# Turning the k scales and the v tiles through VectorE and DRAM instead of TensorE, in a decoder block on one core

## The chip, the cores and the metric

The kernel runs on one core of a Trainium2 chip. The metric is device time in microseconds of one execution, the median of several runs; lower is better. One further execution was recorded by the hardware profiler, and the lines of the profile come from that one.

## The reference

One layer of a hybrid decoder, 512 tokens, model width 2048, all in float32. The input is normalised (RMS) and projected to head groups: A, eight heads of 64 with three causal dilated attention patterns; B, a gated depthwise convolution of 31 taps over 512 channels; C, 16 query heads of 64 on two key/value heads, sliding window of 128, with sinks. In A and C each head's q and k are RMS-normalised. The parts are concatenated, projected and added to the input; a gated feed-forward layer (width 5632) follows.

```python
h = _rms_norm(x, norm1_g[l])
proj = h @ w_in[l]
aq, ak, av, bu, bg, cq, ck, cv = jnp.split(proj, splits, axis=-1)
aq = _rms_norm(aq.reshape(B, S, A_HEADS, HEAD_DIM), a_q_g[l])
ak = _rms_norm(ak.reshape(B, S, A_HEADS, HEAD_DIM), a_k_g[l])
out_a = _dilated_mixture(aq, ak, av).reshape(B, S, A_WIDTH)
...
x = x + mix @ w_out[l]
h2 = _rms_norm(x, norm2_g[l])
x = x + (jax.nn.silu(h2 @ w_gate[l]) * (h2 @ w_up[l])) @ w_down[l]
```

## The kernel before, in words

Activations are kept with the channel on the partition and the 512 tokens along the row. Every float32 product is made of three products of a fast format: operand and weight are each split into a high part (a cast on ScalarE) and a low part (a subtraction on VectorE), and `mm3` (line 314) adds high x high, high x low and low x high.

The work runs in stages. The first four column tiles of the input projection are made together while the input arrives. Then `project` (line 487) makes one tile of 128 columns after another, in the order of `PROJ` (line 46): cv, ck, cq0, bu2, cq3, cq1, and so on to av3, aq3. One tile takes two weight units of 512 KB, eight pairs of 128-row blocks, 48 matmuls of 128x512. The out projection, the gated layer's two input products and its down product follow; the last two are by far the longest part.

Between the matmuls of the projections stands all the attention work. Its place is set by hand: after each pair of blocks `ticks.tick()` is called, and everything that was put down for that tick with `ticks.after(n, ...)` is issued then. A tick is therefore six matmuls and what else of TensorE's work falls into it. Each engine works off its own instructions in the order in which they were issued. All DMAs of this stage are issued from SyncE's queue, in order; an issue that waits (for a buffer to come free, for data) holds those behind it. Weight loads stand in that queue too, up to five units ahead at first and eight later; the casts of a unit are issued two units before its use.

A tile of q or k goes through `head_scales` (line 575): ScalarE copies the projection out of PSUM (line 578) and squares it, VectorE sums the squares by head and turns them in blocks of 32 (line 587), four DMAs write the sums to DRAM (line 595), one reads them back with the tokens on the partitions (line 600), and GpSimd adds and raises to -1/2 (lines 606 to 608). For q that is all: the scale is applied to the scores. For k (`do_k`, line 640) the eight columns of scales are widened by ScalarE to 128x512 (`widen`, line 646), turned by four TensorE transposes into a PSUM bank (`flip`, line 652), multiplied into k by VectorE (`scale`, line 658), split into high and low (lines 663 and 668), and eight DMAs of 128 KB copy the parts of each head to both halves of the partitions (`twin`, line 673). For v (`do_v`, line 680) VectorE multiplies the projection by the tokens' norm factor on its way out of PSUM (line 682), four TensorE transposes bring the tokens onto the partitions (`flip`, line 684), and ScalarE and VectorE split it (`high`, line 690, `low`, line 696).

`attention` (line 716) then puts down a head's scores (line 731), maxima, exponentials, norms, transposes of the weights (lines 769 and 834) and the product with v (`weigh`, line 852). Where a head begins is the latest of several ticks:

```python
t0 = max(ticks.now + ready, head_at[0], box["q at"] - s1, box["k at"], box["v at"] - at_v)
```

`box["k at"]` and `box["v at"]` are fixed numbers of ticks after the tile's projection; they are not measured. cv and ck serve all 16 C heads (first c0, then c3, c1, c5, c2, c7, c4, c6), ak0 to ak3 and av0 to av3 two A heads each.

Of the kernel before, what the change touches and what calls it, by code (L numbers as in the profile page):

```python
# [9 lines left out]
F32 = mybir.dt.float32  # L10
# [4 lines left out]
ALU = mybir.AluOpType  # L15

P = 128
T = 512
NT = T // P
D = 2048  # L20
KT = D // P
HD = 64
HALF = (slice(0, HD), slice(HD, 2 * HD))
# [12 lines left out]
TAP_PAUSE = (197, 211)  # L36


SD, VD, EV = 7, 4, 1


C_TICKS = (1, 6, 2, 2, 2, 3, 5, 1, 4)
# [74 lines left out]
def kernel(ctx: ExitStack, tc: tile.TileContext, xT, wi, wo, wgu, wd, cst_in, outT):  # L117
    nc = tc.nc
    cp = ctx.enter_context(tc.tile_pool(name="consts", bufs=1))
# [16 lines left out]
    ticks = Ticks()  # L136

    def slot(name, dt=F32, cols=T):
        return sp.tile([P, cols], dt, name=name, tag="s")

    def bank(name, cols=T, pool="banks"):
        return psum[pool].tile([P, cols], F32, name=name, tag="b")
# [51 lines left out]
    for p in GU_ORDER:  # L194
        for m in range(2):
# [4 lines left out]
    bufs = {"A": dict(zip(("21", "11", "s", "22"), ("21a", "22a", "sa", "22b"))),  # L200
            "B": dict(zip(("21", "11", "s", "22"), ("21b", "11", "12", "sb")))}
# [6 lines left out]
    for t, (g, r) in enumerate(DOWN):  # L208
# [7 lines left out]
        for k in ("21A", "11A", "21B", "11B", "22A", "22B", "12A", "12B"):  # L216
            c = k[2]
# [20 lines left out]
        bufs = {c: {"21": b["s"], "s": b["21"], "11": b["22"], "22": b["11"]} for c, b in bufs.items()}  # L238

    splits = {}  # L240
    at = {"entry": 0, "split": 0, "use": 0}
# [95 lines left out]
    b = bank("idle")  # L337
    for i in range(WARM):
        nc.tensor.matmul(b, idle, idle[:, None, :].to_broadcast([P, NT, P]), start=True, stop=True)
    b = idle = None  # L340

    nhalf = cp.tile([P, 8], F32, name="nhalf")
# [3 lines left out]
    ident = cp.tile([P, P], F32, name="ident")  # L346
# [28 lines left out]
    gqk = cp.tile([P, 2], F32, name="gqk")  # L375
# [43 lines left out]
    def token_scale(acc, n, name, b=None):  # L419

        v, r = small(name + "v"), small(name + "r")
        if b is None:

            t, b = bank(name), v
            for i in range(NT):
                nc.tensor.transpose(t[:, i * P:(i + 1) * P], acc[:, i * P:(i + 1) * P], ident)
            nc.vector.tensor_reduce(v, t.rearrange("p (a b) -> p a b", b=P), axis=mybir.AxisListType.X, op=ALU.add)
        else:
            stat_rows(b[:, :, None], acc, ones)
        nc.vector.tensor_scalar(v, b, 1.0 / n, EPS, op0=ALU.mult, op1=ALU.add)  # L430
        nc.gpsimd.tensor_tensor(r, v, nhalf[:, :NT], op=ALU.pow)  # L431
        return v, r
# [46 lines left out]
    c64 = cp.tile([P, NT], F32, name="c64")  # L479
    r1b = slot("r1b")  # L480

    v1, r1 = token_scale(ssum, D, "n1")
# [4 lines left out]
    def project(name):  # L487
        b = bank(name, pool="tiles")
        for half in range(2):
            wh, wl = next_unit()  # L490
            for kk in range(8):
                k = 8 * half + kk
                s = slice(kk * P, (kk + 1) * P)
                mm3(b, wh[:, s], wl[:, s], h_hi[k], h_lo[k], k == 0, k == KT - 1)
                if kk == 3:
                    lows_now()
                if kk % 2 == 1:
                    ticks.tick()
        return b
# [72 lines left out]
            mix[f"b{j}"] = yconv[j]  # L572


    def head_scales(b, name, then):

        raw = slot(name + "raw")
        nc.scalar.copy(raw, b)

        def square():  # L580
            sq = slot(name + "sq")
            nc.scalar.activation(sq, raw, AF.Square)
            ticks.after(1, total, sq)

        def total(sq):
            part = cp.tile([P, NT, NT], F32, name=name + "p", tag="hsp", bufs=3)
            nc.vector.tensor_reduce(part.rearrange("p l b -> p b l"),
                                    sq.rearrange("p (b l c) -> p b l c", b=NT, l=NT),
                                    axis=mybir.AxisListType.X, op=ALU.add, apply_transpose=True)
            ticks.after(1, leave, part)  # L590

        def leave(part):
            d = tc.dram_tile([P, 2 * NT * 2], F32, name=name + "d")
            for a in range(4):
                nc.sync.dma_start(d.rearrange("(l i) (a b) -> i l a b", i=32, a=4)[:, :, a], part[32 * a:32 * a + 32])
            ticks.after(2, back, d)

        def back(d):
            t = cp.tile([P, 2, 2, NT], F32, name=name + "t", tag="hst", bufs=3)
            nc.sync.dma_start(t.rearrange("p h a b -> p (h a b)"), d)  # L600
            ticks.after(2, power, t)

        def power(t):
            r = cp.tile([P, NT, 2], F32, name=name + "r", tag="hsr", bufs=4)
            by_head = r.rearrange("p b h -> p h b")
            nc.gpsimd.tensor_add(by_head, t[:, :, 0], t[:, :, 1])
            nc.gpsimd.tensor_add(r, r, c64[:, :, None].to_broadcast([P, NT, 2]))
            nc.gpsimd.tensor_tensor(r, r, nhalf.rearrange("p (a b) -> p a b", b=2), op=ALU.pow)
            then(r)

        ticks.after(1, square)
        return raw
# [25 lines left out]
        ticks.after(1, high)  # L638

    def do_k(box, b, name, gi):  # L640
        def then(r):
            ticks.after(2, widen, r)

        raw = head_scales(b, name, then)
        box["k at"] = ticks.now + SD + 11
        def widen(r):
            wide = slot(name + "wide")
            nc.scalar.copy(wide.rearrange("p (a b c) -> p a b c", a=NT, b=2),
                           r[:, :, :, None].to_broadcast([P, NT, 2, HD]))
            ticks.after(1, flip, wide)  # L650

        def flip(wide):
            b2 = bank(name + "t")
            for i in range(NT):
                nc.tensor.transpose(b2[:, i * P:(i + 1) * P], wide[:, i * P:(i + 1) * P], ident)
            ticks.after(1, scale, b2)

        def scale(b2):
            k = slot(f"{name}k")
            nc.vector.scalar_tensor_tensor(k, raw, gqk[:, gi:gi + 1], b2, op0=ALU.mult, op1=ALU.mult)  # L660
            ticks.after(1, high, k)

        def high(k):
            hi = slot(f"{name}hi", F32R)
            nc.scalar.copy(hi, k)
            ticks.after(1, low, k, hi)

        def low(k, hi):
            lo = slot(f"{name}lo", F32R)
            nc.vector.tensor_sub(lo, k, hi.bitcast(F32))  # L670
            ticks.after(1, twin, hi, lo)

        def twin(*parts):
            box["k"] = [[slot(f"{name}{'hl'[i]}{h}", F32R) for i in range(2)] for h in range(2)]
            for h in range(2):
                for to, part in zip(box["k"][h], parts):
                    for at in HALF:
                        nc.sync.dma_start(to[at].bitcast(F32), part[HALF[h]].bitcast(F32))

    def do_v(box, b, name):  # L680
        vs = slot(name + "s")
        nc.vector.tensor_mul(vs, b, r1b)

        def flip():
            b2 = bank(name + "t")
            for i in range(NT):
                nc.tensor.transpose(b2[:, i * P:(i + 1) * P], vs[:, i * P:(i + 1) * P], ident)
            ticks.after(1, high, b2.rearrange("p (a b c) -> p a b c", a=NT, b=2))

        def high(src):  # L690
            box["v"] = [slot(f"{name}{h}", F32R).rearrange("p (a b c) -> p a b c", a=NT, b=2) for h in range(2)]
            for h in range(2):
                nc.scalar.copy(box["v"][h][:, :, h], src[:, :, h])
            ticks.after(1, low, src)

        def low(src):
            for h, v in enumerate(box["v"]):
                nc.vector.tensor_sub(v[:, :, 1 - h], src[:, :, h], v[:, :, h].bitcast(F32))

        box["v at"] = ticks.now + VD + 3  # L700
        ticks.after(VD, flip)


    UNITS = {
# [240 lines left out]
    for name in PROJ[HEAD4:]:  # L945
# [4 lines left out]
        b = project(name)  # L950
# [3 lines left out]
        if kind == "c":  # L954
            box = Heads(shared) if j else shared
        else:
            box = boxes.setdefault(j, {})
# [10 lines left out]
    b = box = boxes = shared = None  # L968
# [81 lines left out]
    for half in range(2):  # L1050
        for i, n in enumerate(OUT_ORDER[half]):
            if half == 1 and i == 2:
                open_banks(banks=2, high=2)
            b = bank(f"o{half}_{n}", pool="tiles")
            wh, wl = next_unit()
            for kk in range(8):
                k = 8 * half + kk
# [3 lines left out]
                s = slice(kk * P, (kk + 1) * P)  # L1061
# [18 lines left out]
    b = m_hi = m_lo = r1b = mult_a = bias_a = bias_c = over = upper = None  # L1080
# [33 lines left out]
    flip = [1]  # L1114
# [177 lines left out]
    for g in range(2 * NP):  # L1292
        p, m = GU_ORDER[g // 2], g % 2
# [257 lines left out]
```

## Time and profile before

| | |
|---|---|
| Time, median of 3 runs | 1867.45 us (1867.01 to 1867.95) |
| Profiled execution | 1867.59 us |
| Its span, first to last instruction | 1865.9 us |
| TensorE busy | 1858.8 us |
| VectorE, ScalarE, GpSimd busy | 1446.7, 1330.5, 1141.7 us |
| DMA traffic | 307.38 MB, mean 165 GB/s |
| Stage of the projections with attention | about 50 to 480 us of the span |

The times of the rows below count from the start of the span. A row of a timeline has start, duration, engine, line, operation and tile; in brackets stands how long the engine was idle before it and what ended that. In the list of DMAs the last number is the median time from issue to landing in us. In the chain of the work that ended last, a row is a start, a duration and the engine, tile and line that held the chain.

### The profile page before, as it was taken

The numbers are of one execution on the slowest core, as the hardware profiler recorded it, in microseconds if no ns is written. First come the engines' busy times: TensorE is split into PE (matmuls) and PEld (weight loads), VectorE is DVE, ScalarE is ACT, GpSimd is POOL, SyncE is SP. The second block draws the span as 40 slices with busy tenths as digits, with TensorE's granted clock in tenths as the row PEclk, the third lists the DMA queues.
The fourth block names the chain that finished last, engine by engine and source line by source line (L and its number), as shares of the span: only waits on it lengthen the run. The fifth ranks groups of instructions, "written<-read, shape, count | busy, mean of one in ns | idle before, by whom it ended". The sixth has DMA issues, their size and how long they took to land.

```text
span 1865.9 us, 28280 instructions
## 1 busy us (share of the span) xinstructions
PE 1858.8 (100%) x9606; PEld 1591.2 (85%) x9606; DVE 1446.7 (78%) x2290; ACT 1330.5 (71%) x1840; POOL 1141.7 (61%) x828
## 2 busy tenths in 40 slices
PE   9999999999999999999999999999999999999998
PEld 7888888888888888888888888888888888888887
DVE  6778878998689777777777777777777777777777
ACT  6355644553457878888888888888888877778775
POOL 0125533100013877888878878788787878779775
PEclk9999999999999999999999999999999999999999
DMA  7243253343333455555555655555457867677645
GB/s 273 77 145 90 77 147 96 94 130 120 131 123 113 146 160 158 174 183 158 174 158 171 186 155 178 159 171 185 143 168 249 315 226 237 210 228 234 203 131 113
DMA packets 213328, 307.38 MB, mean 165 GB/s; under 512 B 75200, under 2 KB 124992, under 8 KB 213184
## 3 DMA queue, kind: packets, MB, share of 16 engines
q1 hardware_dynamic: 213040, 305.57, 52.3%
q8 instruction: 76, 1.25, 0.3%
q14 instruction: 68, 0.56, 0.1%
q10 hardware_dynamic: 144, 0.01, 0.0%
HBM read 244.03 MB, written 53.09 MB: 159 GB/s over the span
## 4 chain that ended last, share of the span: by engine, by line
PE 99%; DMA 0%; SPq 0%; DVE 0%; issue 0%; ACT 0%; DVEq 0%
PE out L1146 46%; PE out L1405 7%; PE out L1404 7%; PE out L1406 7%; PE o L317 3%; PE o L315 3%; PE o L316 3%; PE cq L315 2%; PE cq L317 2%; PE cq L316 2%; PE ak L315 1%; PE aq L315 1%; PE av L315 1%; PE aq L317 1%; PE aq L316 1%; PE av L316 1%
## 5 line engine op out<-in xcount | busy, mean ns | idle before, releaser
L1146 PE MATMUL out<-h,wh 128*128 128x512 f32 x2464 | 588.5, 391 | 0.0
L1146 PEld LDWEIGHTS out<-h,wh 128*128 128x128 f32 x2464 | 452.7, 188 | 87.5
L1146 PEld LDWEIGHTS out<-h,wl 128*128 128x128 f32 x2464 | 315.9, 191 | 12.0
L1146 PE MATMUL out<-h,wl 128*128 128x256 f32 x2464 | 319.6, 283 | 0.0
L1404 PE MATMUL out<-wh,a 128*128 128x512 f32 x620 | 240.4, 388 | 0.0
L1405 PE MATMUL out<-wl,a 128*128 128x512 f32 x620 | 240.3, 388 | 0.0
L1406 PE MATMUL out<-wh,a 128*128 128x512 f32 x620 | 240.3, 388 | 0.0
L286 ACT CAST wh<-w 128x1024 fp32r<-128x1024 f32 (+2 forms) x94 | 96.8, 1031 | 151.0 <-PE o L316 62.8
L264 DVE TENSOR_TENSOR wl<-w,wh 128x1024 fp32r<-128x1024 f32 (+2 forms) x95 | 113.2, 1191 | 41.1 <-ACT wh L286 39.5
L1404 PEld LDWEIGHTS out<-wh,a 128*128 128x128 f32 x620 | 116.4, 188 | 24.0
L1406 PEld LDWEIGHTS out<-wh,a 128*128 128x128 f32 x620 | 116.4, 188 | 23.8
L1405 PEld LDWEIGHTS out<-wl,a 128*128 128x128 f32 x620 | 116.4, 188 | 23.8
L1414 DVE TENSOR_TENSOR y<-y,out 128x512 f32<-128x512 f32 x164 | 106.2, 683 | 25.7 <-PE out L1406 23.8
L526 DVE SCALAR_TENSOR_TENSOR y<-bu,cst,y 128x511 f32<-128x511 f32 (+14 forms) x120 | 90.0, 750 | 0.7
L315 PE MATMUL o<-mh_c,wh 128*128 128x512 f32 x128 | 51.1, 399 | 0.0
L315 PE MATMUL cq<-hh,wh 128*128 128x512 f32 x128 | 50.5, 395 | 0.0
L317 PE MATMUL o<-mh_c,wl 128*128 128x512 f32 x128 | 50.0, 391 | 0.0
L316 PE MATMUL cq<-hl,wh 128*128 128x512 f32 x128 | 49.9, 390 | 0.0
L316 PE MATMUL o<-ml_c,wh 128*128 128x512 f32 x128 | 49.9, 390 | 0.0
L317 PE MATMUL cq<-hh,wl 128*128 128x512 f32 x128 | 49.9, 390 | 0.0
L431 POOL TENSOR_TENSOR lvr<-lvv,nhalf 128x4 f32<-128x4 f32 x1 | 1.9, 1923 | 70.7 <-DVE lvv L430 70.7
L182 POOL TENSOR_TENSOR w('s', 'g0')_5667<-w('21', 'g0')_5513,w('22', 'g0')_5511 128x1024 f32<-128x1024 f32 x1 | 2.5, 2454 | 69.0 <-DVE wl L264 69.0
(3062 smaller groups left out, 4941.6 us busy)
## 6 DMA issues: line engine op xcount, KB each, us to landing
od<-a SPq DMA_DIRECT2D x154, 256.0 KB, 4.7
a<-od SPq DMA_DIRECT2D x154, 256.0 KB, 5.5
w<-in_wi SPq DMA_DIRECT2D x58, 512.0 KB, 3.5
w<-in_wo SPq DMA_DIRECT2D x32, 512.0 KB, 3.5
x<-in_xT SPq DMA_DIRECT2D x16, 256.0 KB, 7.1
xr<-in_xT SPq DMA_DIRECT2D x16, 256.0 KB, 3.8
x2d<-xr SPq DMA_DIRECT2D x16, 256.0 KB, 2.0
z<-x2d SPq DMA_DIRECT2D x64, 64.0 KB, 3.8
```

The source lines that it names most:

```text
L182: nc.gpsimd.tensor_add(out[:, :n], raws[key[a]][0][:, :n], raws[key[b]][0][:, :n])
L264: fn(*args)
L286: (nc.vector.tensor_copy if u == 0 else nc.scalar.copy)(hi[:, :n], t[:, :n])
L315: nc.tensor.matmul(out, wh, xh, start=start, stop=False)
L316: nc.tensor.matmul(out, wh, xl, start=False, stop=False)
L317: nc.tensor.matmul(out, wl, xh, start=False, stop=stop)
L526: nc.vector.scalar_tensor_tensor(yconv[j][:, i:], hconv[j][:, :T - i], c, yconv[j][:, i:], op0=ALU.mult, op1=ALU.add)
L1146: nc.tensor.matmul(out, lhs[:, s], rhs, start=begin, stop=x is xs[-1] and low == flip[0], skip_group_check=True)
L1404: nc.tensor.matmul(b[:, lo:hi], x[:, high], wh[:, s], start=start, stop=False, skip_group_check=True)
L1405: nc.tensor.matmul(b[:, lo:hi], x[:, high], wl[:, s], start=False, stop=False, skip_group_check=True)
L1406: nc.tensor.matmul(b[:, lo:hi], x[:, low], wh[:, s], start=False, stop=last, skip_group_check=True)
L1414: getattr(eng, op)(t, t, src)
```

## The change

For k, GpSimd writes the eight scales of a token (heads first) into the head of a zeroed 32-column block; VectorE turns that block in pieces of 32x32; four DMAs write the pieces' eight useful rows to DRAM, in rows of 128 bytes, as an array of eight rows of 128 tokens; two DMAs read it back, each one row of 512 tokens of one head spread over 64 partitions. The multiply into k reads that instead of a PSUM bank. From the power to the last copies of k it takes 11 ticks instead of 7, and `box["k at"]` is 21 ticks after the projection instead of 18.

For v, VectorE turns the projection itself in pieces of 32x32 out of PSUM; four DMAs write it to DRAM with tokens as rows, in pieces of 128 bytes; one reads 128x512 back in rows of 512 bytes, and GpSimd multiplies by the norm factor, which now is one number per partition and block. `high` comes seven ticks after the projection instead of five, and `box["v at"]` is ten instead of seven.

All else of the kernel is the same text; lines behind line 575 move by up to 26.

```diff
-SD, VD, EV = 7, 4, 1
+SD, KD, VD, EV = 7, 9, 10, 1
...
         def power(t):
-            r = cp.tile([P, NT, 2], F32, name=name + "r", tag="hsr", bufs=4)
-            by_head = r.rearrange("p b h -> p h b")
-            nc.gpsimd.tensor_add(by_head, t[:, :, 0], t[:, :, 1])
-            nc.gpsimd.tensor_add(r, r, c64[:, :, None].to_broadcast([P, NT, 2]))
-            nc.gpsimd.tensor_tensor(r, r, nhalf.rearrange("p (a b) -> p a b", b=2), op=ALU.pow)
-            then(r)
+            if home is None:
+                r = cp.tile([P, 2, NT], F32, name=name + "r", tag="hsr", bufs=4)
+            else:
+                r = home().rearrange("p (h b) -> p h b", h=2)
+            nc.gpsimd.tensor_add(r, t[:, :, 0], t[:, :, 1])
+            nc.gpsimd.tensor_add(r, r, c64[:, None, :].to_broadcast([P, 2, NT]))
+            nc.gpsimd.tensor_tensor(r, r, nhalf.rearrange("p (h b) -> p h b", h=2), op=ALU.pow)
+            then(r.rearrange("p h b -> p b h"))
...
     def do_k(box, b, name, gi):
+        wide = []
+
+        def home():
+            wide.append(slot(name + "wide"))
+            nc.gpsimd.memset(wide[0][:, 2 * NT:32], 0.0)
+            return wide[0][:, :2 * NT]
+
         def then(r):
-            ticks.after(2, widen, r)
+            ticks.after(2, turn)
-        raw = head_scales(b, name, then)
-        box["k at"] = ticks.now + SD + 11
-        def widen(r):
-            wide = slot(name + "wide")
-            nc.scalar.copy(wide.rearrange("p (a b c) -> p a b c", a=NT, b=2),
-                           r[:, :, :, None].to_broadcast([P, NT, 2, HD]))
-            ticks.after(1, flip, wide)
-
-        def flip(wide):
-            b2 = bank(name + "t")
-            for i in range(NT):
-                nc.tensor.transpose(b2[:, i * P:(i + 1) * P], wide[:, i * P:(i + 1) * P], ident)
-            ticks.after(1, scale, b2)
-
-        def scale(b2):
+        raw = head_scales(b, name, then, home)
+        box["k at"] = ticks.now + SD + KD + 5
+
+        def turn():
+            nc.vector.transpose(wide[0][:, 32:64], wide[0][:, :32])
+            ticks.after(1, leave)
+
+        def leave():
+            d = tc.dram_tile([2 * NT, P], F32, name=name + "e")
+            for a in range(4):
+                nc.sync.dma_start(d[:, 32 * a:32 * a + 32], wide[0][32 * a:32 * a + 2 * NT, 32:64])
+            ticks.after(2, back, d)
+
+        def back(d):
+            rows = d.rearrange("(h b) p -> h (b p)", h=2)
+            for h in range(2):
+                nc.sync.dma_start(wide[0][HALF[h]], rows[h:h + 1].to_broadcast([HD, T]))
+            ticks.after(3, scale)
+
+        def scale():
             k = slot(f"{name}k")
-            nc.vector.scalar_tensor_tensor(k, raw, gqk[:, gi:gi + 1], b2, op0=ALU.mult, op1=ALU.mult)
+            nc.vector.scalar_tensor_tensor(k, raw, gqk[:, gi:gi + 1], wide.pop(), op0=ALU.mult, op1=ALU.mult)
             ticks.after(1, high, k)
...
     def do_v(box, b, name):
-        vs = slot(name + "s")
-        nc.vector.tensor_mul(vs, b, r1b)
-
-        def flip():
-            b2 = bank(name + "t")
-            for i in range(NT):
-                nc.tensor.transpose(b2[:, i * P:(i + 1) * P], vs[:, i * P:(i + 1) * P], ident)
-            ticks.after(1, high, b2.rearrange("p (a b c) -> p a b c", a=NT, b=2))
+        turned = slot(name + "t")
+        nc.vector.transpose(turned, b)
+
+        def leave():
+            d = tc.dram_tile([T, P], F32, name=name + "d")
+            for a in range(4):
+                at = slice(32 * a, 32 * a + 32)
+                nc.sync.dma_start(d.rearrange("(n i) c -> i n c", i=32)[:, :, at],
+                                  turned[at].rearrange("p (n c) -> p n c", c=32))
+            ticks.after(2, back, d)
+
+        def back(d):
+            vs = slot(name + "s")
+            nc.sync.dma_start(vs.rearrange("p (b c) -> p b c", b=NT), d.rearrange("(b p) c -> p b c", p=P))
+            ticks.after(2, scale, vs)
+
+        def scale(vs):
+            by = vs.rearrange("p (a c) -> p a c", a=NT)
+            nc.gpsimd.tensor_mul(by, by, r1[:, :, None].to_broadcast([P, NT, P]))
+            ticks.after(2, high, vs.rearrange("p (a b c) -> p a b c", a=NT, b=2))
...
-        box["v at"] = ticks.now + VD + 3
-        ticks.after(VD, flip)
+        box["v at"] = ticks.now + VD
+        ticks.after(1, leave)
```

2 lines of the change are left out of this document (1 added, 1 removed).

## The prediction

> **What bounds the kernel now.** I read the page first (busy shares, chain that ended last), then what TensorE waited for, then the chain in order of time, and last the timelines of each engine between 55 and 110 us, where the first k and v tiles are made.
>
> ```profile
> PE 1858.8 (100%) x9606; PEld 1591.2 (85%) x9606; DVE 1446.7 (78%) x2290; ACT 1330.5 (71%) x1840; POOL 1141.7 (61%) x828
> ```
> ```profile
> PE 99%; DMA 0%; SPq 0%; DVE 0%; issue 0%; ACT 0%; DVEq 0%
> ```
> ```profile
> PE idle L339 <- DVE ones L349: 1.1, 1, 1.1
> PE sides L1369 <- DVE y L1383: 0.7, 1, 0.7
> PE in L315 <- ACT wh L286: 0.4, 1, 0.4
> ```
>
> TensorE is busy for the whole span and the chain is TensorE for 99% of it. Its only waits are at the two ends; between 60 and 480 us it waits for nothing. So each microsecond of TensorE work that goes is worth a microsecond, and each microsecond for which TensorE is made to wait costs one. All else is cover.
>
> **What is removed.** Ten groups of four transposes (line 655 for five k tiles, line 687 for five v tiles). The chain in order of time prices each; these are the first, the fourth and fifth, and the last of ten:
>
> ```profile
> 68.41 0.44 PE cvt L687 x4
> ```
> ```profile
> 260.78 0.44 PE ak0t L655 x4
> 263.97 0.44 PE av0t L687 x4
> ```
> ```profile
> 389.12 0.44 PE av3t L687 x4
> ```
>
> 10 x 0.44 = **4.4 us less on the path**. The instruction order of the changed kernel has exactly these ten groups fewer and no matmul more. ScalarE also loses a copy per k tile and each v its multiply on VectorE (0.69 us), which a turn of 0.70 us (row below) replaces: both off the path, no gain. The tick times in the order show what moves: the scores of c0 come three ticks later, those of the other early c heads one, from c4 on nothing, and the out projection finds its rows at the same ticks as before.
>
> **What is added.** Per v tile four writes of 64 KB, one read of 256 KB and a GpSimd multiply; per k tile four tiny writes and two reads of 128 KB: 55 issues. They cost SyncE some 25 us at the 0.44 us of a row below. Its queue has cover in general:
>
> ```profile
> SPq L254 <- DVE wl L264: 827.8, 194, 11.0
> ```
>
> What counts is whether a chain of DMAs ends later than TensorE needs it. TensorE needs a k tile first at c0, after cv and ck, where a tick is shortest (no attention work between the matmuls):
>
> ```profile
> 98.43 0.39 PE L315 MATMUL cq<-hh,wh 128*128 128x512 f32 x1
> 98.66 0.39 PE L316 MATMUL cq<-hl,wh 128*128 128x512 f32 x1
> ```
> ```profile
> 99.11 0.22 PE L737 MATMUL c0s<-ckh,cq 128*128 128x128 f32 x1
> 99.17 0.28 PE L738 MATMUL c0s<-ckl,cq 128*128 128x128 f32 x1
> ```
>
> Matmuls start 0.227 us apart, six make a tick: 1.36 us. Three ticks later and two groups of transposes (cv, ck) earlier, c0's scores come up at 99.1 + 4.1 - 0.9 = **102.3 us**. I follow the two chains to that moment.
>
> *The v tile of cv.* In the new order on ScalarE its two casts stand ahead of the copy of ck's projection, and wait for GpSimd's multiply, that for the read, that for the writes.
>
> ```profile
> L1267 DVE STREAM_TRANSPOSE zt<-z x16: 703/704/705, 714.0 to 1298.5; 128x512 f32<-128x512 f32 x16
> ```
> ```profile
> 65.12 0.69 DVE L682 TENSOR_TENSOR cvs<-cv,r1b 128x512 f32<-128x512 f32 x1
> ```
> ```profile
> 89.32 0.74 DVE L660 SCALAR_TENSOR_TENSOR ckk<-ckraw,gqk,ckt 128x512 f32<-128x512 f32 x1
> ```
> ```profile
> 92.44 0.69 DVE L670 TENSOR_TENSOR cklo<-ckk,ckhi 128x512 fp32r<-128x512 f32 x1
> ```
> ```profile
> 68.89 0.65 ACT L693 CAST cv<-cvt 128x256 fp32r<-128x256 f32 x2 [0.93 <-PE cvt L687]
> 73.00 0.59 ACT L578 COPY ckraw<-ck 128x512 f32<-128x512 f32 x1 [3.46 <-PE ck L317]
> ```
> ```profile
> 59.79 2.55 POOL L517 TENSOR_TENSOR bu<-bu,bg 128x512 f32<-128x512 f32 x2 [7.54 <-ACT bg L516]
> ```
> ```profile
> 84.61 1.64 POOL L608 TENSOR_TENSOR ckr<-ckr,nhalf 128x8 f32<-128x8 f32 x1
> ```
> ```profile
> 88.21 1.75 SPq L595 DMA_DIRECT2D cq0d<-cq0p  x4
> 90.01 0.53 SPq L636 DMA_DIRECT2D cq<-cq0l  x1
> 90.58 0.59 SPq L637 DMA_DIRECT2D cq<-cq0l  x1
> ```
> ```profile
> 93.94 1.48 SPq L678 DMA_DIRECT2D ckl<-cklo  x2
> ```
> ```profile
> w<-in_wi SPq DMA_DIRECT2D x58, 512.0 KB, 3.5
> ```
> ```profile
> x2d<-xr SPq DMA_DIRECT2D x16, 256.0 KB, 2.0
> z<-x2d SPq DMA_DIRECT2D x64, 64.0 KB, 3.8
> ```
> ```profile
> y<-x2t SPq DMA_DIRECT2D x16, 256.0 KB, 6.9
> ```
> ```profile
> ckh<-ckhi SPq DMA_DIRECT2D x4, 128.0 KB, 2.8
> ckl<-cklo SPq DMA_DIRECT2D x4, 128.0 KB, 2.7
> ```
>
> The turn stands where the multiply stood: 65.1 to 65.8. Four issues at 0.44 us, the last begun at 67.2. The trace has no such write; the nearest row is z, the same 64 KB in pieces of 128 bytes, four issues in a row, the other way: 3.8 us, so landed at 71.0. The 256 KB read is not in the trace either; between x2d's 2.0 and y's 6.9 the nearest is a weight tile, a DRAM read in this very stage: 3.5 us, landed at 74.5. The multiply takes half of 2.55: 75.8. The casts take 0.65: 76.5. ScalarE could have taken ck's copy at 73.0, so **ck starts 3.5 us late**. Two weight loads are held back behind them on SyncE, by some 5 us; the row above shows such waits of up to 11.0 us that TensorE never felt, so that costs nothing.
>
> *The k tile of ck.* Its square, sum, first trip through DRAM and power stay as they are, so the power ends at 86.25 + 3.5 = 89.8. The turn of 32 columns (between nothing and 0.7; I take 0.2) ends at 90.0. On SyncE follow four writes (1.75), the four of cq0 queued behind them (1.75), the two of line 636/637 (1.15, by their starts and the last's length) and two reads, the second begun at 95.2. 128 KB with 2 KB rows is ckh's row, 2.8 us: **98.0**. VectorE wanted it at tick 31: the old line 655 stood at tick 26, 87.8, so 87.8 - 0.4 + 5 x 1.36 = 94.2. VectorE waits, and behind it stand a gated input, a weight's low half and a tap; unit 21's low half is wanted at tick 40 only. From ckk to the end of cklo the trace has 3.8 us with the same sort of work between (89.32 to 93.13): 101.8. Then two issues of 0.6, the second at 102.5, and 2.7 to land: **105.2**. TensorE stands at c0 since 102.3 and waits **2.9 us**. That is the cost; it isn't made good later, as nothing else bounds the kernel.
>
> *The other eight tiles* I cost at nothing. Ticks last 1.6 us and more there (ak0t at tick 130 and av0t at tick 132 stand 3.2 us apart above), so 6 and 7 ticks give the same chains 10 us; the k tiles wait 7 to 71 ticks for their scores after their last copies, against 3 at ck. The tightest place I found is a0's product with av0, where ak1's low half and av1's two now fall among the VectorE work ahead of it:
>
> ```profile
> 333.79 0.42 DVE L850 TENSOR_TENSOR a0pl<-a0t,a0ph 128x256 fp32r<-128x256 f32 x1
> ```
> ```profile
> 334.92 0.28 PE L864 MATMUL a0o<-a0pl,av 128*128 128x256 f32 x1
> ```
>
> 0.7 us of slack, against some 0.6 us of work moved in (net of what moves out before an idle stretch): 0 to 0.5 us, I take 0.
>
> **Sum.** -4.4 + 2.9 = -1.5. The profiled execution took 1867.59 (span 1865.9 and 1.7 around it), 0.14 above the median of 1867.45; from the median: **1866.0 us**, 0.08% less. About 0.2% (3.7 us) is what a measurement of this kernel can tell from no change.
>
> **Rivals.**
>
> *No wait at c0: 1863.0.* If the v tile's write and read both take x2d's 2.0 us, 3.3 us of the 3.5 go, and with them all 2.9 of the wait; the full 4.4 remain: 1867.45 - 4.4. For it: by the DMA line of the page the second slice (47 to 93 us) is at 0.2, while z and y ran after 700 us, at 0.4 to 0.8. Against it: 512 pieces per write.
>
> ```profile
> DMA  7243253343333455555555655555457867677645
> ```
> Every wait under 0.7 us gives a time that counts as faster.
>
> *The v tile comes much later: 1870.8 to 1872.8, slower.* One place, the queue of ScalarE behind cv's casts. The price is what the two transfers take beyond my values: z's slowest took 5.2 (row below), y's median is 6.9, so 1.4 + 3.4 = 4.8 more: the wait is 7.7, the sum +3.3, 1870.8. It decides from a wait of 8.1 us, that is, from c0's low half landing at 110.4. A dropped clock (next) would add 2.0.
>
> ```profile
> DMA to landing us min/median/max: 3.3/3.8/5.2
> ```
>
> *The wait also drops TensorE's clock: 1868.0.* The trace has TensorE coming out of idleness at its start:
>
> ```profile
> 1.12 3.56 PE L339 MATMUL idle<-idle 128*128 128x512 bf16 x8 [1.12 <-DVE ones L349]
> 4.55 1.47 PE L472 MATMUL in<-hh,wh 128*128 128x512 f32 x4
> ```
>
> Eight matmuls at 0.43 us apart and four at 0.33, against 0.227: 8 x 0.2 + 4 x 0.1 = 2.0 us lost. The same after a wait at c0 gives 1866.0 + 2.0. [...]
>
> *That the change does not do what it says* I leave no chance: the transposes are gone from the order.
>
> **How the numbers follow.** Forecast (wait of 0.7 to 7 us, clock kept) 0.54; no wait 0.26; late v 0.12; dropped clock 0.08. Faster by over 0.2%: 0.26. Slower: 0.12. Within: 0.54 + 0.08 = 0.62. The range goes from no wait, 1863.0, to the late v at full clock, 1871.0; beyond lie parts of the late v (0.1) and extra gain or loss that I can't name.
>
> **What would show it.** TensorE's waits should have one new row, c0's scores (line 763) for a DMA of ckl or ckh, about 2.9 us, and its first score near 105. ck's copy on ScalarE (line 578) should start near 76.5 behind a wait of the casts for GpSimd. The landing of cvd and cvs tests 3.8 and 3.5, that of ckwide 2.8. ckk (line 674) should start near 98.0. TensorE's groups should be ten fewer, the granted clock 1.0 and matmuls after c0 0.227 apart. I am wrong if TensorE waits elsewhere (a0's product, line 890, first), or if ScalarE takes ck's copy at 73 all the same.

## The result, and the profile after

The changed kernel takes **1874.75 us** (median of 7 runs, 1870.12 to 1877.69), the kernel before 1867.45 on the same chip: a ratio of 1.0038, with a 95% interval of 1.0027 to 1.005. The forecast was 1866.0 with a range up to 1871.0; the time lies above it, 7.3 us slower. The profiled execution took 1874.93 with a span of 1873.2, which is 7.3 more than the span of before, so it can stand for the median.

Two lines of its page answer to those of before: busy time of the engines, and the chain that ended last.

```profile
PE 1857.4 (99%) x9566; PEld 1588.8 (85%) x9566; DVE 1449.9 (77%) x2295; ACT 1327.3 (71%) x1835; POOL 1155.5 (62%) x838
...
PE 89%; DVE 5%; DMA 2%; SPq 2%; POOL 1%; issue 1%; ACT 0%; POOLq 0%; DVEq 0%
```

Forty matmul records fewer, as said. But the chain is no longer TensorE alone: a tenth of the span now passes through the other engines, DMAs and SyncE's queue. What TensorE waited for (us in total, times, longest):

```profile
PE o L315 <- DVE xr L1019: 2.5, 2, 1.6
PE c7o L890 <- POOL c7pl L822: 2.1, 2, 1.8
PE c4o L890 <- POOL c4pl L822: 1.8, 2, 1.3
PE c6s L763 <- DMA cq<-cq6l: 1.2, 1, 1.2
PE idle L339 <- DVE ones L349: 1.1, 1, 1.1
PE a1o L890 <- DVE a1pl L876: 1.0, 1, 1.0
PE sides L1395 <- DVE y L1409: 0.7, 1, 0.7
PE c0s L764 <- DMA ckl<-cklo: 0.6, 1, 0.6
```

Rows for `idle` and `sides` are the old ones at the ends. The other six are new: nine waits, 9.2 us. The one that I had forecast, c0's, is the smallest. The large ones stand at products of the c heads (c7o, c4o), at c6's scores and at the out projection, between 250 and 430 us, and none of them waits for a tile that the change makes. So something behind the changed tiles was late. VectorE's waits show the first candidate, a wait for a tile's own trip through DRAM, which the kernel before doesn't make:

```profile
DVE ckk L674 <- DMA ckwide<-cke: 3.9, 1, 3.9
...
DVE ak0k L674 <- DMA ak0wide<-ak0e: 3.5, 1, 3.5
...
DVE ak2k L674 <- DMA ak2wide<-ak2e: 2.8, 1, 2.8
```

In these rows VectorE takes its instructions in order. The multiply into k stands in its queue, and while it waits for the DRAM read, all behind it waits too, other heads' work above all: c7lp below starts at 242.48, though its input c7hp was done on ScalarE at 239.00 and VectorE stood idle for 2.75 us in between. Around ak2 (start, length, idle time before in brackets):

```profile
232.74 0.21 DVE L657 STREAM_TRANSPOSE ak2wide<-ak2wide 128x32 f32<-128x32 f32 x1 [0.90 <-POOL ak2wide L610]
...
237.47 1.48 DVE L526 SCALAR_TENSOR_TENSOR y<-bu,cst,y 128x483 f32<-128x483 f32 x2
241.69 0.75 DVE L674 SCALAR_TENSOR_TENSOR ak2k<-ak2raw,gqk,ak2wide 128x512 f32<-128x512 f32 x1 [2.75 <-DMA ak2wide<-ak2e]
242.48 0.69 DVE L810 TENSOR_TENSOR c7lp<-c7t,c7hp 128x512 fp32r<-128x512 f32 x1
```

From the turn to the landed read it is 9.0 us; VectorE had 6.2 us of other work between the two and then stood 2.75. Right behind stands the low half of c7's weights, c7lp. GpSimd makes c7ph and c7pl of c7's halves, and c7o is the next thing TensorE waits for after c0, at 251.79. (The step between the two is looked at below.)

At ak0 the delay goes on to SyncE. The multiply started at 271.53 after 3.45 of idleness. Behind it on VectorE stand the low half of a weight (274.54), for which a weight load on SyncE waits 6.4 us, and ak0's own low half (276.33). So the eight twin transfers of ak0 (line 692) are issued only from 276.23 on, in one run, and cq6's transfers stand behind them, though their sums were ready at 277.63. c6's scores wait for these:

```profile
268.77 7.36 SPq L254 DMA_DIRECT2D w<-in_wi  x2
276.23 1.12 SPq L692 DMA_DIRECT2D ak0h<-ak0hi  x2
...
280.52 1.10 SPq L692 DMA_DIRECT2D ak0l<-ak0lo  x2
281.72 2.28 SPq L595 DMA_DIRECT2D cq6d<-cq6p  x4
284.11 0.47 SPq L638 DMA_DIRECT2D cq<-cq6l  x1
```

### The profile page after: what moved, and what is told of

It is laid out like the page before. It is cut to its first block, busy times and chain, and to the rows that moved or that the text cites. A ratio compares the mean times of both kernels' runs of the same rounds, so it can differ in the third digit from the quotient of the medians.

```text
span 1873.2 us, 28281 instructions
## 1 busy us (share of the span) xinstructions
PE 1857.4 (99%) x9566; PEld 1588.8 (85%) x9566; DVE 1449.9 (77%) x2295; ACT 1327.3 (71%) x1835; POOL 1155.5 (62%) x838
## 4 chain that ended last, share of the span: by engine, by line
PE 89%; DVE 5%; DMA 2%; SPq 2%; POOL 1%; issue 1%; ACT 0%; POOLq 0%; DVEq 0%
PE out L1172 46%; PE out L1431 7%; PE out L1430 7%; PE out L1432 7%; PE o L315 3%; PE o L317 3%; PE o L316 3%; PE cq L315 1%; PE cq L317 1%; PE cq L316 1%; DVE wl L264 1%; PE in L315 1%; PE in L317 1%; PE in L316 1%; DVE y L526 1%
```

## The experiments

My theory after this, **W**: engines that take their work in order stand waiting for the new DRAM reads, and what is queued behind them, other heads' steps, comes too late for TensorE. The rival **Q**: the 55 issues and their traffic delay other transfers wherever they stand, waits or not. Later came **S** (slots) and **T** (the c heads' shifted ticks). Every kernel ran beside the kernel before on the same chip, whose median there was 1867.4 to 1867.6; the ratio is to that, with its 95% interval.

| run | what it is | us | ratio to before |
|---|---|---|---|
| (changed) | | 1874.75 | 1.0038 (1.0027 to 1.0050) |
| no_turn | before, transposes left out | 1862.29 | 0.9973 (0.9962 to 0.9984) |
| later | changed, A tiles read later | 1865.81 | 0.9993 (0.9984 to 1.0002) |
| k_late | changed, A's k tiles read later | 1866.75 | 0.9999 (0.9991 to 1.0008) |
| v_late | changed, A's v tiles read later | 1873.05 | 1.0029 (1.0020 to 1.0038) |
| k_only | k half of the change | 1870.63 | 1.0018 (1.0009 to 1.0027) |
| v_only | v half of the change | 1866.54 | 0.9994 (0.9986 to 1.0003) |
| extra | before + 55 idle transfers, two slots held | 1876.22 | 1.0045 (1.0031 to 1.0058) |
| extra_t | the same, no slot held | 1869.00 | 1.0007 (0.9998 to 1.0016) |
| slots71 | before with 71 slots | 1869.39 | 1.0010 (1.0001 to 1.0018) |
| ck_te | changed, ck on TensorE | 1873.64 | 1.0033 (1.0022 to 1.0045) |
| a02_te | changed, ak0 and ak2 on TensorE | 1868.47 | 1.0007 (0.9998 to 1.0016) |
| a13_te | changed, ak1 and ak3 on TensorE | 1872.34 | 1.0028 (1.0018 to 1.0038) |
| twin_late | changed, ak1's and ak3's twins later | 1878.53 | 1.0061 (1.0048 to 1.0073) |
| mix | 28 of 40 transposes gone | 1863.88 | 0.9981 (0.9972 to 0.9990) |
| mix_all | 36 of 40 gone | 1869.14 | 1.0010 (1.0001 to 1.0019) |

### later, k_late, v_late: more ticks before the read's user

```diff
 # do_k, A tiles only
-            ticks.after(3, scale)
+            ticks.after(7, scale)
 # do_v, A tiles only
-            ticks.after(2, scale, vs)
+            ticks.after(6, scale, vs)
...
-            ticks.after(2, high, vs...)
+            ticks.after(4, high, vs...)
```

`later` has both edits, `k_late` the first, `v_late` the second; `box["k at"]` and `box["v at"]` move along, and so do the casts and twins behind the multiply.

> The changed kernel with more ticks between a transfer's issue and the instruction that reads it, for the eight tiles of the A heads alone (k: three ticks become seven; v: two become six, and two become four ahead of the casts). Same instructions, same 55 issues. Theory W (engines that take their work in order stand waiting for the DRAM reads: VectorE 2.8 us for ak2wide and 3.5 us for ak0wide, ScalarE 4.3 us behind av0s, and the other heads' steps queued behind them come late): these waits go, and with them TensorE's at c7o, c4o, a1o and the output projection (7.4 us of its 9.2): 1863 to 1867 us. Theory Q (the issues themselves, on SyncE's queue and as DMA traffic, delay other heads' transfers wherever they stand): as the changed kernel, 1870 to 1877.

> The changed kernel with the later multiply (three ticks become seven) for the four k tiles of the A heads alone; v as changed. Tells which of the two kinds of wait made the 8.9 us that the run with both later won. If it is VectorE's wait for ak0wide and ak2wide (6.2 us of idle, with the P halves of c7 and c4 queued behind): most of it, 1866 to 1868 us. If it is ScalarE's and GpSimd's wait at the v tiles: 1872 to 1875. If the two add up to one (each shifts the other's transfers on SyncE): in between, 1868 to 1872.

> The counterpart: later multiply and casts for the four v tiles of the A heads alone; k as changed. If VectorE's wait at k is the cause: VectorE still stands 2 to 4 us at ak2wide and ak0wide, 1871 to 1874 us. If v's is: 1866 to 1868. If shared: 1868 to 1872.

Measured: 1865.81, 1866.75, 1873.05. As W has it: 8.9 us come back with the same 55 issues in place, 8.0 of them by the k tiles' multiply alone. (The times of `later` and `k_late` themselves cannot be told from before's: both intervals include 1.) `later`'s waits of TensorE:

```profile
PE c0s L766 <- DMA ckl<-cklo: 1.6, 1, 1.6
PE idle L339 <- DVE ones L349: 1.1, 1, 1.1
PE a1s L766 <- DMA ak1l<-ak1lo: 1.0, 1, 1.0
PE sides L1397 <- DVE y L1411: 0.7, 1, 0.7
PE a3s L765 <- DMA ak3h<-ak3hi: 0.6, 1, 0.6
```

c7o, c4o, c6s, a1o and o are gone from it. In their place a1 and a3 wait for their own k tiles, which four more ticks bring too late: these heads have no slack. Since the casts and the twins of A's k tiles move too, the time alone doesn't part VectorE's wait from a better place of the twins on SyncE; the rows have to do that.

The step from VectorE's 2.8 us to c7o's 1.8 goes by a detour on GpSimd. cq4's row landed within 0.4 us of the same moment in both kernels; then in the changed one

```profile
243.39 0.29 POOL L608 TENSOR_TENSOR cq4r<-cq4t 128x8 f32<-128x8 f32 x1 [7.59 <-DMA cq4t<-cq4d]
243.76 2.91 POOL L609 TENSOR_TENSOR cq4r<-cq4r,c 128x8 f32<-128x8 f32 x1
...
252.50 0.29 POOL L822 TENSOR_SCALAR_AFFINE_SELECT c7pl<-c7lp 128x128 fp32r<-128x128 f32 x1
```

and in `later`

```profile
243.74 0.20 POOL L608 TENSOR_TENSOR cq4r<-cq4t 128x8 f32<-128x8 f32 x1 [7.68 <-DMA cq4t<-cq4d]
244.02 0.20 POOL L609 TENSOR_TENSOR cq4r<-cq4r,c 128x8 f32<-128x8 f32 x1
...
249.38 0.73 POOL L824 TENSOR_SCALAR_AFFINE_SELECT c7pl<-c7lp 128x128 fp32r<-128x128 f32 x1
```

an addition of eight numbers per partition takes 2.91 us instead of 0.20, and c7pl ends 2.7 us later (252.8 against 250.1). In the changed kernel VectorE was just then working off what had piled up, without a gap from 241.69 on; in `later` it was idle for 1.7 us before 244.94. In the kernel before and in `k_late` VectorE was idle during this addition as well, and it takes 0.20 there too. Why it takes 2.91 beside a busy VectorE, no run shows. Over the kept traces, c7o waits in three kernels alone, the changed one, `v_late` and `k_only`, and in these GpSimd's three instructions for cq4's row take 4.8, 4.5 and 3.8 us, in all others 2.0 to 3.1. In `a13_te` and `twin_late` VectorE stands 2.2 and 2.3 us at ak2 too, but the row takes 2.1 and 2.2 and c7o does not wait. So c7o waits by way of GpSimd; that VectorE's backlog is what held GpSimd up is argued, as no run took the two apart.

c4o's wait has a part of another kind. Ahead of its first piece of c4pl GpSimd stood 2.66 us:

```profile
277.19 0.41 POOL L819 TENSOR_SCALAR_AFFINE_SELECT c4pl<-c4lp 128x256 fp32r<-128x256 f32 x1 [2.66 <-PE c4t L799]
```

It reads c4lp, which was ready at 274.62, and nothing of c4t, so what it stood for is the slot that c4t's input held. In `slots71`, where nothing differs but two missing slots, the same line (for another piece) stands 2.36 us for the same transposes. So the slots that the change's tiles hold have a share in c4o's 1.8 us; `later`, `k_late` and `a02_te` have neither this wait nor c4o's.

### k_only, v_only: each half alone

The other half's functions and ticks are those of the kernel before.

```diff
 # k_only: do_v of before (its flip after 4 ticks); v_only: do_k of before
```

> The k half of the change alone: 30 of the 55 issues, half of the transposes gone (2.2 us). Theory W: VectorE's three long waits (2.8, 3.5 and 3.9 us) are all for k's reads, so most of the loss comes back: 1869 to 1873 us. Theory Q: 30/55 of the 11.9 us that the changed kernel lost beside what it saved, less 2.2: 1867.45 + 6.5 - 2.2 = 1871.7.

> The v half alone: 25 of the 55 issues, the other half of the transposes gone (2.2 us). Theory W: no VectorE wait for a read is left, only ScalarE's and GpSimd's (4.3 us at av0): 1865 to 1868 us. Theory Q: 25/55 of 11.9 us less 2.2: 1867.45 + 5.4 - 2.2 = 1870.7.

Measured 1870.63 and 1866.54. `v_only` fits W alone; `k_only` fits W and Q (1871.7) alike. The k half is the loss, the v half at best a small gain (1.0 of the 2.6 us that its transposes are worth, and its interval includes no change). But 3.1 and -1.0 make 2.1, not 7.3: the halves make each other worse. `k_only`'s waits of VectorE point at one place:

```profile
DVE ak2k L674 <- DMA ak2wide<-ak2e: 2.1, 1, 2.1
...
DVE ak0k L674 <- DMA ak0wide<-ak0e: 1.1, 1, 1.1
```

ak0's wait is 1.1 us without v tiles, 3.5 with: in the changed kernel av0's four writes stand ahead of ak0's four on SyncE (issued from 262.01 and 264.38). This is a likely reason and not a shown one: with the same v tiles ak0's wait was only 1.7 to 2.1 in `ck_te`, `a13_te` and `twin_late`.

### no_turn: what the transposes are worth

```diff
-            b2 = bank(name + "t")
-            for i in range(NT):
-                nc.tensor.transpose(b2[...], wide[...], ident)
-            ticks.after(1, scale, b2)
+            ticks.after(1, scale, wide)
 # and the same in do_v
```

> The kernel before without the 40 transposes and with nothing in their place: VectorE and ScalarE read the unturned tiles from where they lie, at the same ticks. It leaves out the turning itself, and its output is not the reference's. It prices the removal alone: 40 x 0.11 us = 4.4 us of TensorE, so 1863.0 us if TensorE is the bound where they stand; 1867.4 if their time is given back in a wait.

Measured 1862.29, 5.3 us below before (1867.57 there) and 0.7 below what was expected: some 0.13 us per transpose, and nothing is given back in a wait. (In its trace the matmuls of the projections gain 0.47 us on the kernel before at each of the ten groups, 4.7 in all.) So the changed kernel lost 1874.75 - 1862.29 = 12.5 us to its own chains.

### extra, extra_t, slots71: the transfers by themselves

```diff
 # extra: in do_k and do_v of before, at the ticks of the change
+            nc.sync.dma_start(d[...], src[...])          # four writes
+            nc.sync.dma_start(dst[...], ...)             # one read, two for k
 # extra_t: src is the constant bias_a, and
+            dst = slot(name + "x")                       # for each read
 # slots71
-N_SLOTS = 73
+N_SLOTS = 71
```

> The kernel before, transposes and all, plus the change's 55 transfers of the same shapes at the same ticks on SyncE, between a scratch slot and DRAM: nobody reads what they bring. Theory W (only instructions that wait for a transfer cost): TensorE's path is untouched, 1867 to 1869 us. Theory Q (the issues and the traffic cost by themselves): the 11.9 us that the changed kernel lost beside its saving, or the larger part of it: 1873 to 1879 us.

> The kernel before plus the change's 55 transfers for nobody, as in the earlier run of that kind, but without the two scratch slots that run held all along: the writes leave from a constant tile, and each read lands in a slot taken for it alone and free when it has landed. In the earlier run GpSimd stood 8.3 us for a slot that ak0lo's twin transfers (issued 5 us later than in the kernel before) had not freed. Theory S (the two slots made that wait, the issues are free): 1867 to 1869 us. Theory Q (the issues delay the twins, and whoever comes next in a slot waits for them): 1872 to 1877.

> The control: the kernel before with 71 slots for 73, no transfer added. Theory S: most of the 8.7 us of the earlier run with 55 idle transfers, 1872 to 1876. Theory Q: 1867 to 1868.

`extra` at 1876.22 seemed to prove Q. It didn't. GpSimd stood for a slot that ak0's twins held, and TensorE behind it:

```profile
280.50 0.45 POOL L822 TENSOR_SCALAR_AFFINE_SELECT c4pl<-c4lp 128x256 fp32r<-128x256 f32 x1 [8.30 <-DMA ak0l<-ak0lo]
```

Without the two held slots the same 55 transfers cost 1.6 us (interval -0.4 to 3.0), and two slots fewer without any transfer cost 2.0. Neither alone is 8.7; together they are. The row above suggests why: a transfer that is late is harmless until the next user of its slot is near (here GpSimd, which stood 8.30 us for it). For `slots71` both forecasts missed (S too high, Q too low), for `extra_t` S's upper end held. So the issues are nearly free, as forecast, as long as nobody waits for them, and Q doesn't make the loss of the changed kernel. S as such doesn't either, as two slots cost 2.0 us; but what the changed kernel's own extra slots (one more per v tile while it turns) add to it was not tried, and c4o's row above suggests that they add something.

### ck_te, a02_te, a13_te: single tiles back on TensorE

```diff
-            do_k(box, b, name, 1 if kind == "c" else 0)
+            (do_k if name in NAMES else do_k_dram)(box, b, name, 1 if kind == "c" else 0)
 # do_k is that of before, do_k_dram the changed one; NAMES: ck | ak0 ak2 | ak1 ak3
```

> The changed kernel with ck alone back on TensorE, so that the c heads stand at the ticks of the kernel before; 36 transposes gone. Theory W (VectorE's waits for ak2wide and ak0wide): these stay, 1870 to 1874 us. Rival T (the c heads' shift by one to three ticks put c7's P halves behind cq4's row on GpSimd and so made the loss): c7o, c4o and c6s no longer wait, 1865 to 1868.

> The changed kernel with ak0 and ak2 back on TensorE (32 transposes gone); ck, ak1, ak3 and all v tiles as changed. The changed kernel's TensorE waits at c7o, c4o and c6s (5.1 of 9.2 us) stand right behind VectorE's waits for ak2wide and ak0wide. If these two waits are their cause: 5.1 x 11.9/9.2 = 6.6 us come back, 0.9 us of transposes return, 1869 us (1868 to 1870), and o and a1o still wait. If the c waits have another cause (the v tiles, the c heads' ticks): 1873 to 1876.

> The counterpart: ak1 and ak3 back on TensorE, ck, ak0, ak2 and the v tiles as changed. If the waits of o and a1o (3.5 us of 9.2) come from ak1's and ak3's later steps (their twins' issues, 6 us of SyncE, now stand ahead of the read of aq3's row, and VectorE stands 3.5 us for that row): 4.5 us come back, 0.9 return, 1871 us (1870 to 1872), and c7o, c4o, c6s still wait. If o and a1o wait because VectorE is behind since ak2 and ak0: 1874 to 1876.

Measured 1873.64, 1868.47, 1872.34: the first two land in their forecasts, the last one just beside it, and T falls as the cause of the loss (c7o's wait alone is gone in `ck_te`). Going back on ak0 and ak2 wins 6.3 us though eight transposes return, on ak1 and ak3 2.4, on ck 1.1; the last two gains are within the intervals, so for ak1 and ak3 the rows have to speak. In `a02_te` no c head waits but c0, and o and a1o still do (2.0 and 0.6 us); in `a13_te` o and a1o no longer wait, and c4o and c6s do (0.9 and 1.7; c7o is spared this time). So the c heads' waits go with ak0 and ak2, those of o and a1o with ak1 and ak3. (One execution each: that of `a02_te` took 1871.26 us, 2.8 above its median, and its wait of 2.00 us at c0 was followed by a granted clock of 0.71 over 4 us, see the last section.) The shares overlap (with the v half's 4.1 they make more than the loss), so they are not a sum.

### mix, mix_all, twin_late: the best version, and a second queue

```diff
 # mix: all v tiles, cv too, with later's ticks, ak0 and ak2 as in later, ck, ak1, ak3 on TensorE
 # mix_all: also ak1 and ak3 through DRAM, scale one tick later
 # twin_late: the changed kernel, ak1 and ak3 only
-            ticks.after(1, twin, hi, lo)
+            ticks.after(4, twin, hi, lo)
```

> All five v tiles through DRAM with the later multiply and casts, of the k tiles only ak0 and ak2 (whose heads start 15 and more ticks after the k tile is due), with the later multiply; ck, ak1 and ak3, whose heads wait for them, on TensorE as before. 28 of 40 transposes gone. Theory W: no in-order wait and no head that waits for its k tile (the run with both later still lost 3.2 us at c0, a1 and a3): 1867.5 less 28/40 of the 5.3 us that the run without turning won = 1863.8, so 1863 to 1865 us. Theory Q: 25 + 12 = 37 issues cost 37/55 of 11.9 us = 8.0, so 1871.8.

> All v tiles through DRAM with the later multiply and casts, the k tiles of the four A heads through DRAM (ak0 and ak2 four ticks later, ak1 and ak3 one), ck on TensorE: 36 of 40 transposes gone. Theory W: 1867.5 less 36/40 of 5.3 us = 1862.7, and up to 1.6 more if a1 and a3 wait for their k tiles as with four ticks (1.0 and 0.6 us): 1862.5 to 1864.5. Theory Q: 20 + 4 x 6 + 5 = 49 issues by 0.2 us each above that, 1872.

> The changed kernel with ak1's and ak3's twin transfers alone issued three ticks later, so behind aq1's and aq3's reads of their rows. If the twins' place ahead of those reads makes VectorE's 3.5 us wait at a3d and TensorE's 2.5 us at o: these go, 1871 to 1872.5 us, or, if the twins then land after a1 and a3 begin, up to 2 us of it comes back there (a1s, a3s): 1871 to 1874. If not: 1874 to 1876 and o waits as before.

`mix` measured **1863.88**, where W said 1863.8. It is the best version: 3.6 us under the kernel before (the interval ends at 0.9990), and TensorE waits at the ends alone:

```profile
PE idle L339 <- DVE ones L349: 1.1, 1, 1.1
PE sides L1437 <- DVE y L1451: 0.7, 1, 0.7
```

`mix_all` missed: 1869.14 for 1862.7. VectorE waits for no DRAM read of the change there (GpSimd does, 10.0 us for cvs and 6.0 for av2s, but 10.1 and 9.3 in `mix`, at no cost), so W as I had put it was not all. Its difference from `mix` is seen at aq3. In `mix` SyncE issues the read of aq3's row, VectorE uses the row:

```profile
403.44 0.33 SPq L600 DMA_DIRECT2D aq3t<-aq3d  x1
```
```profile
410.31 0.16 DVE L874 SCALAR_TENSOR_TENSOR a3d<-a3d,aq3r 128x2 f32<-128x2 f32 x1 [0.73 <-POOL aq3r L610]
```

In `mix_all` ak3's eight twin issues, six microseconds of SyncE, have come in between:

```profile
401.92 1.18 SPq L733 DMA_DIRECT2D ak3h<-ak3hi  x2
...
408.12 1.42 SPq L600 DMA_DIRECT2D aq3t<-aq3d  x1
```
```profile
414.84 0.16 DVE L874 SCALAR_TENSOR_TENSOR a3d<-a3d,aq3r 128x2 f32<-128x2 f32 x1 [5.12 <-POOL aq3r L610]
```
```profile
421.01 0.47 PE L315 MATMUL o<-mh_c,wh 128*128 128x512 f32 x1 [3.21 <-DVE xr L1061]
```

VectorE stands 5.12 us for the row, the residual addition behind it frees a PSUM bank late, and TensorE stands 3.21 us in the out projection. It is the same fault on another queue: nobody waits for a new transfer, but a moved step's issues stand ahead of an old one. The changed kernel has a milder form (twins at 403.54 to 409.6, the row's read at 414.15, VectorE idle 3.49 us for it). `twin_late` was to take the twins behind that read and failed at it: three ticks put them between the row's write and its read, the read moved on to 418.42, VectorE's idleness to 4.01, and the time went up by 3.8 us, past all its forecasts. But TensorE's wait at o for VectorE did not grow (2.1 us, 2.5 in the changed kernel); the new waits are those of a1's and a3's scores, 2.5 us, mostly for the late twins themselves, and the granted clock dropped behind c6s's wait (2.04 us, then 0.59 over 4 us) and o's (2.10, then 0.69). So it neither confirms nor refutes the reading of aq3's row, and that twins behind the read would be free was not shown. Of the places tried none was good for ak1 and ak3: earlier the twins delay the row, later (as in `later`) the heads wait.

## Why the prediction was wrong

*TensorE is the bound, and the transposes' 4.4 us come off it*: right, with 5.3 for 4.4 by the times of `no_turn` and 4.7 by its trace.

*The tick times: c heads three or one later, out projection the same*: right as an order, and not the cause of the loss (`ck_te` wins 1.1 us).

*The issues, 25 us of SyncE, lie under its cover*: right for issues that nobody waits for (`extra_t`, 1.6 us), wrong for their order. I had counted SyncE's time and not asked who stands behind an issue that itself waits, or behind the twins, which move with the k tile although their number stays.

*cv's chain, ck 3.5 us late*: too long. The writes had landed when the read was issued at 69.35 (forecast 71.0), the read had landed at 72.3 (74.5), and ck's copy followed the casts at once, 1.0 us late and not 3.5:

```profile
73.40 0.71 ACT L719 CAST cv<-cvs 128x256 fp32r<-128x256 f32 x2 [5.53 <-POOL cvs L713]
74.02 0.58 ACT L578 COPY ckraw<-ck 128x512 f32<-128x512 f32 x1
```

*ck's chain, a wait of 2.9 us at c0*: the mechanism was right, the size not. TensorE came to c0 at 102.2, as forecast (102.3). VectorE did stand at ckk, from 92.3 to 96.21 (forecast 94.2 to 98.0, so already here it was there ahead of the ticks), and c0's scores for ckl, 0.6 us:

```profile
102.98 0.30 PE L764 MATMUL c0s<-ckl,cq 128*128 128x128 f32 x1 [0.60 <-DMA ckl<-cklo]
```

In kernels with the same ck chain that wait was 0.2 to 2.0, so 2.9 lay above them all. The term was too large; with its right size the forecast would have been lower still.

**The step that failed** is the next: *the other eight tiles I cost at nothing, since 6 and 7 ticks of 1.6 us and more give the same chains 10 us*. The chain's 9.0 us was about right. The 10 us were not there: a tick is a place in VectorE's order, no time. VectorE goes on as soon as its inputs are there; at ak2 the turn came late (GpSimd's power took 2.66 us and VectorE stood 0.90 for it), what lies between was only 6.2 us of work, and VectorE arrived early and stood 2.75. At ck I had named what is queued behind the waiting multiply; at ak0 and ak2 I only asked whether the tiles' own heads had slack, which a0 and a2 had, and what work moves in ahead of a0's product, not whose work stands behind a waiting multiply. The loss falls on c7, c4 and c6. That it comes from these two tiles is shown: `k_late` and `a02_te` win 8.0 and 6.3 us back. The steps between are read from the rows: GpSimd at c7o (argued in part), SyncE at c6s, and at c4o a slot as well. The out projection and a1o are the second part, ak1's and ak3's twins on SyncE (`a13_te`, 2.4 us net).

*The sum.* From the measured parts: -5.3, c0's wait 0.6, the other new waits 8.6, together +3.9 of the 7.3 us. Part of the rest lies in how a wait is shown: it begins when the last matmul ends, not when the next could have started. At c7o:

```profile
249.70 0.28 PE L889 MATMUL c7o<-c7ph,cv 128*128 128x256 f32 x1
251.79 0.39 PE L890 MATMUL c7o<-c7pl,cv 128*128 128x256 f32 x1 [1.81 <-POOL c7pl L822]
252.01 0.28 PE L889 MATMUL c7o<-c7ph,cv 128*128 128x256 f32 x1
252.13 0.28 PE L890 MATMUL c7o<-c7pl,cv 128*128 128x256 f32 x1
```

From 249.70 to 251.79 are 2.09 us where two such matmuls usually start 0.12 apart, so 1.97 are lost and 1.81 shown. The two traces tell the rest, when the starts of the same projection matmuls are set against each other. The changed kernel falls back by 2.6 us at c7o (2.1 shown as waits), 2.6 at c4o (1.8), 1.4 at c6s (1.2), 1.1 at a1o (1.0) and 2.9 at the out projection (2.5): 10.6 us for 8.6 shown. With 0.6 at c0 and the 4.7 that the ten groups give in a trace, that is +6.5 of the 7.3 us; the remaining 0.8 lies in small steps.

*The rivals.* None had this mechanism. The slower one had the right kind of fault, an engine that stands in order for a DRAM read, but the wrong place (ScalarE behind cv, where nothing was lost), and its own price, 1870.8, was within the 3.7 us that were to count as no change. That it said slower is no merit of it.

The dropped clock was a rival at c0 with a price of 2.0 us. The price was taken from the start of the span, where the matmuls start 0.43 us apart; but the profile of before has a granted clock of 1.00 from 0 to 9 us, so those rows show no dropped clock, and the chance of 0.08 rested on no run. In the changed kernel's profile the granted clock is 1.00 throughout. In others it did fall, to 0.50 to 0.71 over 4 us, mostly behind waits of 2.00 us and more (last section).

## What to carry to other kernels

When a step that reads on chip becomes a trip through memory, look first at the engine that will take the result: it stood in order here (VectorE 2.75 us at ak2 and 3.45 at ak0), and what it held up was what was queued behind it, whoever that belonged to. Slack counted in the tile's own consumers says nothing about that; put the user of the read so late in its engine's order that the engine never arrives first, and count the issues that move along, and what stands behind them on their queue. Where the consumer has no such slack, leave the tile on the old path: here 28 of 40 transposes gone gave a gain, 36 a loss, and 40 a loss or, with the later reads, no clear change.

## What the runs showed of the hardware

In some of the kernels TensorE's granted clock fell behind a wait. `extra`, after a wait of 3.10 us that ended at 282.35 and one of 0.60 that ended at 283.70, in stretches of 4 us: length, then busy time and instructions of TensorE, its weight loads, VectorE, ScalarE and GpSimd, then granted clock, DMA share and GB/s.

```profile
280.00:284.00 4.00, 1.04 (x5) 0.84 (x6) 3.14 (x5) 1.26 (x2) 2.45 (x4) 0.89 0.50 87
284.00:288.00 4.00, 4.00 (x12) 3.23 (x12) 1.69 (x3) 0.58 (x1) 3.21 (x7) 0.50 0.34 123
288.00:292.00 4.00, 4.00 (x17) 3.30 (x16) 0.53 (x1) 1.53 (x2) 1.87 (x5) 0.76 0.00 0
292.00:296.00 4.00, 4.00 (x21) 3.34 (x20) 2.55 (x7) 1.01 (x2) 0.00 (x0) 1.00 0.40 131
```

The clock is 0.50 there, and the matmuls start 0.42 us apart, not 0.23 as behind it:

```profile
285.36 0.63 PE L317 MATMUL aq<-hh,wl 128*128 128x512 f32 x1
285.78 0.63 PE L315 MATMUL aq<-hh,wh 128*128 128x512 f32 x1
...
291.86 0.39 PE L316 MATMUL ak<-hl,wh 128*128 128x512 f32 x1
292.09 0.40 PE L317 MATMUL ak<-hh,wl 128*128 128x512 f32 x1
```

From 284.4 to 289.6 that is twelve matmuls by 0.2 us, 2.4 us lost on top of the waits. The same came after waits of 3.21 (`mix_all`, 0.59 in the 4 us behind it), 2.00 at c0 (`a02_te`, 0.71) and 1.4 with a second short one (`k_only`, 0.58), and did not after 1.97 at c0 (`k_late`) and 1.81 at c7 (changed kernel), all 1.00. It came after each of the other waits of 2.0 us and more (`v_late` 2.27, clock 0.67; `a13_te` 2.03, 0.61; `twin_late` 2.04 and 2.10, 0.59 and 0.69) and not after 1.58 at o (changed kernel), 1.61 at c0 (`later`) and 1.7 at c6s (`a13_te`), all 1.00. Of two shorter waits close together, `k_only`'s 1.4 and 0.3 had it, while 1.81 and 0.31 in the changed kernel and 1.4 and 0.5 in `v_late`, all at c7o, had not; why was not tested. So in these runs a single wait of 2.00 us was enough, and one of 1.97 was not. A wait near 2 us cost its length, or its length and some 1.6 us: an estimate from `a02_te`, where behind the wait eight matmuls from 105.63 to 109.01 start 0.42 us apart and not 0.23. That may be part of the wide spread of the changed kernel's runs (1870.12 to 1877.69, against 1866.54 to 1867.95 before): the profiled executions of `a02_te` and `k_only`, with a dropped clock, took 1871.26 and 1873.62 us against medians of 1868.47 and 1870.63, that of `k_late`, without, 1866.36 against 1866.75. No kernel has two profiles to compare.
